# Attention scores of two heads requested together, with the keys' low halves multiplied on 64 partitions each

## The chip, the cores and the metric

One core of one Trainium2 chip runs the whole program as a single launch. The metric is the device time of one execution in microseconds (us). The kernel before was run three times: 1482.33, 1476.66 and 1482.65 us, median 1482.33. One further execution was profiled.

## What is computed

The reference is one step of a two-layer trunk on 128 context tokens and 1024 latent tokens, model width 1024. Each layer normalises, modulates and projects its input, feeds three branches (A attention, B gated mixing, C DeltaNet scan), and projects the joined result back. The change lies in branch A:

```python
def _attend(q, k, v, mask, sink):
    s = jnp.einsum('bqhgd,bkhd->bhgqk', q, k).astype(jnp.float32) * (HEAD_DIM ** -0.5)
    s = jnp.where(mask, s, NEG_INF)
    m = jnp.maximum(jnp.max(s, axis=-1, keepdims=True), sk)   # sk: one logit per head
    p = jnp.exp(s - m)
    p = p / (jnp.sum(p, axis=-1, keepdims=True) + jnp.exp(sk - m))
    return jnp.einsum('bhgqk,bkhd->bqhgd', p.astype(v.dtype), v)
```

There are 8 query heads of 64 dimensions on 2 key heads. A block of 128 latent queries sees its own block of keys, its two neighbours and 128 cached context keys, so up to 512 keys; a context query sees the 128 context keys.

## The kernel before, in words

Tokens are nine tiles of 128 (eight latent, one context, `CTX`). Products that need more than half precision are made from halves: a float32 value is split into a float16 high part and a float16 remainder (the low part).

In `attention`, each key head `kv` and each token tile `t` is a unit. `prep` projects the four query heads of the tile (the helper `proj_tok`, line 170, 24 matmuls for each of queries and gates), rotates them, splits them into halves (ACT copies the high half, line 916, and POOL subtracts for the low half, line 917), and a DMA transposes them (line 919), so that in `qT[:, h, :]` a head's high half stands on partitions 0 to 63 and its low half on 64 to 127. `put_k` has stored the keys the same way but with each half doubled: `Kh` holds the high half on both groups of 64 partitions, `Kl` the low half on both. Hence `qT`·`Kh` over 128 partitions gives (q high + q low)·k high in one matmul, and `qT`·`Kl` gives (q high + q low)·k low.

`heads` takes the four heads in turn. Per head there are one or two blocks of keys (128, or 128 plus 256 or 384), and per block one matmul with `Kh` (line 941) and one with `Kl` (line 942) into the same PSUM bank; head 0 and 2 use bank `b` (`psb`), head 1 and 3 bank `a` (`psa`). Then DVE adds the mask and takes the row maximum (line 946), ACT makes the exponentials (lines 948 and 949), POOL the low half of the probabilities (line 951), and a DMA on SP's queue transposes them (line 953). `weigh` multiplies them with the values five heads later (line 967).

There are two layers, two key heads, nine tiles and four heads: 144 heads, 272 key blocks. The order on each engine is made ahead of time by the tile scheduler, which lists instructions by priority (place in the program) and by when it reckons their inputs ready; each engine then works its list strictly in that order. The program interleaves the attention with the scan of branch C by estimated costs (`merge`). Much of the scan runs on parts of the TensorE array: lines 566 to 597 use 64 by 64 of it, lines 527 and 543 use 32 by 32, and the modulation weights (line 249) use 128 rows by 32 columns. The projections, scores and `weigh` use all 128 by 128.

Of the kernel before, what the change touches and what calls it, by code (L numbers as in the profile page):

```python
# [15 lines left out]
ALU = mybir.AluOpType  # L16
# [30 lines left out]
def hybrid_trunk(  # L47
# [9 lines left out]
    V, S_, G, T = nc.vector, nc.scalar, nc.gpsimd, nc.tensor  # L57
# [8 lines left out]
    def pool(name, bufs=1, side=None):  # L66
        return tc.tile_pool(name=name, bufs=bufs, side=side, reuse_waits="tile")
# [9 lines left out]
    def nm(s):  # L77
        ngen[0] += 1
        return f"{s}_{ngen[0]}"

    def bank(tag, bufs, cols=512, dt=F32):
        return psm.tile([128, cols], dt, tag=tag, name=nm("ps"), bufs=bufs)

    def psp():
        return bank("p", 3)

    def psa(cols=512, dt=F32):
        return bank("a", 1, cols, dt)

    def psb(cols=512, dt=F32):  # L90
        return bank("b", 1, cols, dt)
# [73 lines left out]
    def proj_tok(ps, t, wg, c0=0, n=256):  # L165

        i = 0
        for k in range(8):
            for (a, b) in ((0, 0), (0, 1), (1, 0)):
                T.matmul(ps, X[:, t, k, a, :], wg[:, k, b, c0:c0 + n], start=(i == 0), stop=(i == 23))  # L170
                i += 1
# [691 lines left out]
    def rope_tile(rp, src, nh, rt):  # L863

        n = nh * 64
        a = rp.tile([128, 256], F32, tag="ra", name=nm("ra"), bufs=1)
        u = rp.tile([128, 256], F32, tag="ru", name=nm("ru"), bufs=1)
        s3 = src.rearrange("p (h d) -> p h d", d=64)
        V.tensor_tensor(a[:, 0:n].rearrange("p (h d) -> p h d", d=64), s3, bc(rt[:, 0:64], 1, nh), op=ALU.mult)
        V.tensor_tensor(u[:, 0:n].rearrange("p (h d) -> p h d", d=64), s3, bc(rt[:, 64:128], 1, nh), op=ALU.mult)  # L870
        a4 = a[:, 0:n].rearrange("p (g s f) -> p g s f", s=2, f=16)
        u4 = u[:, 0:n].rearrange("p (g s f) -> p g s f", s=2, f=16)
        V.tensor_tensor(a4[:, :, 0, :], a4[:, :, 0, :], u4[:, :, 1, :], op=ALU.add)
        V.tensor_tensor(a4[:, :, 1, :], a4[:, :, 1, :], u4[:, :, 0, :], op=ALU.add)
        return a

    def attention(l, other=iter(())):
        with pool(f"t3{l}", 1, "right") as p1:
            KT = p1.tile([128, 2, 2, 1280], F16, name="KT")
            Kh, Kl = KT[:, 0], KT[:, 1]  # L880
# [23 lines left out]
            def prep(p2, kv, t, wq, wa):  # L904
                pq = psp()
                proj_tok(pq[:, 0:256], t, wq)
                proj_tok(pq[:, 256:512], t, wa)
                rt = p2.tile([128, 128], F32, tag="rt", name=nm("rt"))
                dma(rt, rope[t])
                qa = rope_tile(p2, pq[:, 0:256], 4, rt)  # L910
                th = p2.tile([128, 256], F32, tag="ga", name=nm("ga"), bufs=5)
                S_.activation(th, pq[:, 256:512], AF.Tanh, scale=IWS * 0.5)
                V.scalar_tensor_tensor(th, th, 1.0, pq[:, 256:512], op0=ALU.add, op1=ALU.mult)
                ql = p2.tile([128, 4, 2, 64], F16, tag="ql", name=nm("ql"))
                q3 = qa.rearrange("p (h d) -> p h d", d=64)
                S_.copy(ql[:, :, 0, :], q3)
                G.tensor_tensor(ql[:, :, 1, :], q3, ql[:, :, 0, :], op=ALU.subtract)
                qT = p2.tile([128, 4, 128], F16, tag="qT", name=nm("qT"), bufs=3)
                turn(qT, ql.rearrange("p h s d -> p (h s d)"))
                return qT, th  # L920

            def heads(p2, prev, kv, t, qT, th):
                if t == CTX:
                    blocks, mk = [(9, 1)], am[:, 0:128]
                else:
                    lo, hi = max(t - 1, 0), min(t + 1, 7)
                    blocks = [(lo, hi - lo + 1), (8, 1)] if t == 0 else [(8, 1), (lo, hi - lo + 1)]
                    mk = am[:, 256:640] if t == 0 else (am[:, 0:384] if t == 7 else am[:, 0:512])
                blist = [b + i for (b, n) in blocks for i in range(n)]
                nk = 128 * len(blist)  # L930
                sm = p2.tile([128, 4], F32, tag="sm", name=nm("sm"), bufs=4)
                nmx = p2.tile([128, 4], F32, tag="nmx", name=nm("nmx"), bufs=4)
                box = []
                for h in range(4):
                    hh = 4 * kv + h
                    ps = psa() if h % 2 else psb()
                    c0 = 0
                    for (b, n) in blocks:
                        cs = slice(c0, c0 + 128 * n)
                        ks = slice(128 * b, 128 * (b + n))  # L940
                        T.matmul(ps[:, cs], qT[:, h, :], Kh[:, kv, ks], start=True, stop=False)  # L941
                        T.matmul(ps[:, cs], qT[:, h, :], Kl[:, kv, ks], start=False, stop=True)  # L942
                        c0 += 128 * n
                    sS = p2.tile([128, 512], F32, tag="sS", name=nm("sS"))
                    P16 = p2.tile([128, 1024], F16, tag="P16", name=nm("P16"), bufs=4)
                    V.tensor_tensor_reduce(sS[:, 0:nk], ps[:, 0:nk], mk, -0.125, nsk[:, hh:hh + 1], ALU.add, ALU.min,  # L946
                                           accum_out=nmx[:, h:h + 1])
                    S_.activation(P16[:, 0:nk], sS[:, 0:nk], AF.Exp, bias=nmx[:, h:h + 1], scale=-1.0)  # L948
                    S_.activation(sS[:, 0:nk], sS[:, 0:nk], AF.Exp, bias=nmx[:, h:h + 1], scale=-1.0,  # L949
                                  accum_out=sm[:, h:h + 1])  # L950
                    G.tensor_tensor(P16[:, nk:2 * nk], sS[:, 0:nk], P16[:, 0:nk], op=ALU.subtract)  # L951
                    PT = p2.tile([128, 8, 128], F16, tag="PT", name=nm("PT"), bufs=AHEAD)
                    turn(PT[:, 0:2 * len(blist), :], P16[:, 0:2 * nk])
                    last = (kv, t, th, sm, nmx) if h == 3 else None
                    pend.append((p2, prev, box, kv, h, blist, PT, last))
                    if len(pend) > AHEAD - 1:
                        weigh(*pend.pop(0))
                    yield 0.95

            def weigh(p2, prev, box, kv, h, blist, PT, last):  # L960

                if not box:
                    box.append(bank("o", 1))
                pops, nb = box[0], len(blist)
                mm = [(0, 0, 128)] + [(j, 1, 64) for j in range(nb)] + [(j, 0, 128) for j in range(1, nb)]
                for i, (j, a, n) in enumerate(mm):
                    T.matmul(pops[:, 128 * h:128 * h + n], PT[:, a * nb + j, :],  # L967
                             Vt[:, blist[j], kv].rearrange("p s d -> p (s d)")[:, 0:n], start=(i == 0), stop=(i == len(mm) - 1))
                if h == 1 and prev:
                    finish(p2, *prev.pop())  # L970
                if last is not None:
                    normal(p2, prev, pops, *last)
# [31 lines left out]
            for kv in range(2):  # L1004
                with pool(f"t3b{l}{kv}", 2, "right") as p2:
                    if kv == 0:
# [7 lines left out]
                        for t in ordert:  # L1014
                            ps = psp()
# [16 lines left out]
                    for i in range(NT + 1):  # L1032
                        if i < NT:
                            ready.append((kv, ordert[i], *prep(p2, kv, ordert[i], wq, wa)))
                            yield 5.2
                        if i > 0:
                            yield from heads(p2, prev, *ready.pop(0))
                            if next(other, None) is not None:
                                yield 3.5
# [104 lines left out]
    for l in range(NL):  # L1144
# [13 lines left out]
        c0 = rs.enter_context(pool(f"c0{l}", 1, "right"))  # L1158
# [116 lines left out]
```

## Time and profile before

| | |
|---|---|
| median of three runs | 1482.33 us (1476.66 to 1482.65) |
| the profiled execution, its own time | 1485.41 us |
| its span, first to last instruction | 1483.6 us |
| mean granted TensorE clock | 0.937 of full speed |
| busy: PE, PEld, DVE, ACT, POOL | 89, 68, 63, 42 and 41% of the span |
| score matmuls, lines 941 and 942 | 272 each, from 243.2 to 1342.1 us |

PE is TensorE's matmul, PEld its weight load. A matmul's shown duration contains its way through the pipeline, so matmuls in a row overlap in the rows; what a matmul costs the engine is the distance from its start to the next one's start. The chain that ended last is followed back from the last instruction; a line's share in it is the time for which that line set the pace.

### The profile page before, as it was taken

The numbers are of one execution on the slowest core, as the hardware profiler recorded it, in microseconds if no ns is written. First come the engines' busy times: TensorE is split into PE (matmuls) and PEld (weight loads), VectorE is DVE, ScalarE is ACT, GpSimd is POOL, SyncE is SP. The second block draws the span as 40 slices with busy tenths as digits, with TensorE's granted clock in tenths as the row PEclk, the third lists the DMA queues.
The fourth block names the chain that finished last, engine by engine and source line by source line (L and its number), as shares of the span: only waits on it lengthen the run. The fifth ranks groups of instructions, "written<-read, shape, count | busy, mean of one in ns | idle before, by whom it ended". The sixth has DMA issues, their size and how long they took to land.

```text
span 1483.6 us, 38268 instructions
## 1 busy us (share of the span) xinstructions
PE 1319.0 (89%) x15479; PEld 1014.8 (68%) x15479; DVE 939.3 (63%) x2230; ACT 618.9 (42%) x1411; POOL 610.7 (41%) x818
## 2 busy tenths in 40 slices
PE   6899989799999699859897999999898769987997
PEld 2765576576768597648786655678787658765786
DVE  3865689885565676554446587687775485666333
ACT  2733444424555226632343444332476313664111
POOL 0751245424655235633232432631667403675200
PEclk8999999997999799969997999999999879998999
DMA  9331045736884218673332122242277212666443
GB/s 362 108 85 47 23 117 112 161 93 151 188 182 93 57 44 150 113 211 78 116 130 78 36 69 60 90 92 51 51 138 132 47 49 69 134 116 169 122 162 107
DMA packets 301564, 162.94 MB, mean 110 GB/s; under 512 B 212622, under 2 KB 277938, under 8 KB 301386
## 3 DMA queue, kind: packets, MB, share of 16 engines
q1 hardware_dynamic: 301261, 160.45, 44.7%
q8 instruction: 122, 2.00, 0.6%
q14 instruction: 56, 0.46, 0.1%
q10 hardware_dynamic: 125, 0.04, 0.0%
HBM read 95.78 MB, written 24.28 MB: 81 GB/s over the span
## 4 chain that ended last, share of the span: by engine, by line
PE 54%; DVE 17%; DMA 13%; issue 7%; POOL 6%; ACT 3%; SPq 1%; DVEq 0%; POOLq 0%; ACTq 0%
PE ps L170 15%; PE ps L1072 12%; PE ps L312 7%; DMA PT<-P 4%; DVE sv L510 2%; DVE sv L512 2%; POOL P L951 2%; PE ps L967 2%; DMA st<-in_w_in_dram 2%; PE ps L249 1%; PE ps L543 1%; DMA st<-in_w_mod_dram 1%; PE ps L527 1%; PE ps L941 1%; DVE y L319 1%
## 5 line engine op out<-in xcount | busy, mean ns | idle before, releaser
L170 PEld LDWEIGHTS <-X 128*128 128x128 f16 x3888 | 349.2, 100 | 106.2 <-issue 43.6
L170 PE MATMUL ps<-wg,X 128*128 128x256 f16 x2592 | 327.3, 279 | 9.1 <-DVE wg L161 3.3
L1072 PEld LDWEIGHTS <-OTm 128*128 128x128 f16 x1728 | 170.0, 100 | 39.9 <-DMA OTm<-mix_d 15.8
L951 POOL TENSOR_TENSOR P<-sS,P 128x512 f16<-128x512 f32 (+2 forms) x144 | 148.9, 1040 | 100.0 <-ACT sS L949 99.4
L1072 PE MATMUL ps<-wo,OTm 128*128 128x256 f16 x1296 | 155.5, 279 | 15.5 <-DMA OTm<-mix_d 14.9
L312 PE MATMUL ps<-X,wg 128*128 128x512 f16 (+1 forms) x864 | 144.8, 326 | 1.8 <-ACT wg L160 1.4
L946 DVE CUSTOM_DVE_ANT_0 sS<-ps,am,nsk 128x512 f32<-128x512 f32 (+2 forms) x144 | 95.0, 670 | 43.7 <-POOL P L951 27.3
L170 PE MATMUL ps<-wb,X 128*128 128x256 f16 x864 | 105.4, 284 | 17.7 <-ACT wb L160 16.8
L312 PEld LDWEIGHTS <-wg 128*128 128x128 f16 x864 | 73.0, 98 | 68.5 <-ACT wg L160 1.8
L948 ACT ACTIVATE P<-sS,nmx 128x512 f16<-128x512 f32 (+2 forms) x144 | 93.4, 659 | 61.5 <-DVE nmx L946 61.0
L949 ACT ACTIVATE sS<-sS,nmx 128x512 f32<-128x512 f32 (+2 forms) x144 | 94.8, 658 | 3.2
L145 POOL TENSOR_TENSOR rs<-ms,mhalf 128x1 f32<-128x1 f32 x36 | 20.6, 574 | 174.8 <-DVE ms L1081 104.3
L967 PE MATMUL ps<-Vt,PT 128*128 128x128 f16 (+1 forms) x992 | 68.2, 212 | 20.7 <-DMA PT<-P 19.6
L319 DVE SCALAR_TENSOR_TENSOR y<-zT,cw,y 128x1156 f32<-128x1156 f32 x48 | 68.9, 1439 | 27.8 <-ACT y L317 27.2
L512 DVE TENSOR_TENSOR sv<-sv 128x31 f32<-128x31 f32 (+15 forms) x186 | 76.2, 410 | 4.2
L967 PEld LDWEIGHTS <-PT 128*128 128x128 f16 x992 | 51.1, 101 | 38.8 <-DMA PT<-P 28.2
L510 DVE TENSOR_TENSOR sv<-sv 128x31 f32<-128x31 f32 (+15 forms) x186 | 74.9, 403 | 4.1
L942 PE MATMUL ps<-KT,qT 128*128 128x128 f16 (+2 forms) x272 | 68.8, 271 | 0.0
L941 PE MATMUL ps<-KT,qT 128*128 128x128 f16 (+2 forms) x272 | 60.6, 273 | 7.1 <-DVE nmx L946 2.9
L1075 ACT ACTIVATE sq<-ps 128x512 f32<-128x512 f32 x36 | 21.4, 595 | 105.8 <-PE ps L1072 64.1
L288 DVE TENSOR_SCALAR hf<-ps,AB 128x128 f32<-128x128 f32 x117 | 39.7, 402 | 39.6 <-PE ps L281 39.5
L161 DVE SCALAR_TENSOR_TENSOR wg<-st,wg 128x1024 f16<-128x1024 f32 x44 | 56.4, 1292 | 12.3 <-ACT wg L160 12.2
(265 smaller groups left out, 2730.0 us busy)
## 6 DMA issues: line engine op xcount, KB each, us to landing
st<-in_w_in_dram SPq DMA_DIRECT2D x40, 512.0 KB
st<-in_w_mod_dram SPq DMA_DIRECT2D x32, 512.0 KB
OTm<-mix_d SPq DMA_DIRECT2D x18, 512.0 KB
wm<-in_w_mod_dram SPq DMA_DIRECT2D x16, 512.0 KB
xt<-in_x_sample_dram SPq DMA_DIRECT2D x16, 512.0 KB
st<-in_w_out_dram SPq DMA_DIRECT2D x16, 512.0 KB
mix_d<-OTA SPq DMA_DIRECT2D x36, 128.0 KB
xs<-xt SPq DMA_DIRECT2D x9, 512.0 KB
```

Of the source, the lines that this page charges most:

```text
L170: T.matmul(ps, X[:, t, k, a, :], wg[:, k, b, c0:c0 + n], start=(i == 0), stop=(i == 23))
L312: T.matmul(ps[:, 0:n], wg[:, k, b, 128 * hg:128 * hg + 128], X[:, t0:t1, k, a, :], start=(i == 0), stop=(i == 23))
L319: V.scalar_tensor_tensor(y, zT[:, tap:tap + 1156], cw[:, tap * 6 + ct:tap * 6 + ct + 1], y, op0=ALU.mult, op1=ALU.add)
L510: V.tensor_tensor(t3, m3[:, 0:m, m:m + 1].to_broadcast([128, m, w]), y3[:, m:m + 1, m:32].to_broadcast([128, m, w]), op=ALU.mult)
L512: V.tensor_tensor(y3[:, 0:m, m:32], y3[:, 0:m, m:32], t3, op=ALU.subtract)
L941: T.matmul(ps[:, cs], qT[:, h, :], Kh[:, kv, ks], start=True, stop=False)
L946: V.tensor_tensor_reduce(sS[:, 0:nk], ps[:, 0:nk], mk, -0.125, nsk[:, hh:hh + 1], ALU.add, ALU.min, accum_out=nmx[:, h:h + 1])
L948: S_.activation(P16[:, 0:nk], sS[:, 0:nk], AF.Exp, bias=nmx[:, h:h + 1], scale=-1.0)
L949: S_.activation(sS[:, 0:nk], sS[:, 0:nk], AF.Exp, bias=nmx[:, h:h + 1], scale=-1.0, accum_out=sm[:, h:h + 1])
L951: G.tensor_tensor(P16[:, nk:2 * nk], sS[:, 0:nk], P16[:, 0:nk], op=ALU.subtract)
L967: T.matmul(pops[:, 128 * h:128 * h + n], PT[:, a * nb + j, :], Vt[:, blist[j], kv].rearrange("p s d -> p (s d)")[:, 0:n], start=(i == 0), ...
L1072: T.matmul(ps[:, 256 * i:256 * i + 256], OTm[:, k, a, :], w[:, k, b, :], start=(n == 0), stop=(n == 23))
```

## The change

The scores of heads `h` and `h + 1` are now written together for `h` = 0 and 2, both PSUM banks taken at once. The products with the keys' high halves stay as they are, over 128 partitions. The product with the low halves now takes q high alone: head `h` uses partitions 0 to 63, head `h + 1` partitions 64 to 127, so that each occupies half the rows of the array and all of its columns (64 by 128). For that the odd heads' halves are stored the other way round in `ql`, so line 916's one copy and line 917's one subtraction become two each, half as wide. The product of q low with k low is left out.

```diff
-                S_.copy(ql[:, :, 0, :], q3)
-                G.tensor_tensor(ql[:, :, 1, :], q3, ql[:, :, 0, :], op=ALU.subtract)
+                for i in range(2):
+                    S_.copy(ql[:, i::2, i, :], q3[:, i::2])
+                    G.tensor_tensor(ql[:, i::2, 1 - i, :], q3[:, i::2], ql[:, i::2, i, :], op=ALU.subtract)
...
-                    ps = psa() if h % 2 else psb()
-                    c0 = 0
-                    for (b, n) in blocks:
-                        cs = slice(c0, c0 + 128 * n)
-                        ks = slice(128 * b, 128 * (b + n))
-                        T.matmul(ps[:, cs], qT[:, h, :], Kh[:, kv, ks], start=True, stop=False)
-                        T.matmul(ps[:, cs], qT[:, h, :], Kl[:, kv, ks], start=False, stop=True)
-                        c0 += 128 * n
+                    if h % 2 == 0:
+                        pss = [psb(), psa()]
+                        c0 = 0
+                        for (b, n) in blocks:
+                            cs = slice(c0, c0 + 128 * n)
+                            ks = slice(128 * b, 128 * (b + n))
+                            for i in range(2):
+                                T.matmul(pss[i][:, cs], qT[:, h + i, :], Kh[:, kv, ks], start=True, stop=False)
+                            for i in range(2):
+                                hf = slice(64 * i, 64 * i + 64)
+                                T.matmul(pss[i][:, cs], qT[hf, h + i, :], Kl[hf, kv, ks], start=False, stop=True)
+                            c0 += 128 * n
+                    ps = pss[h % 2]
```

The scheduler places these matmuls one by one, and what it makes of a pair is seen in TensorE's order. First place: layer 0, a latent tile with key blocks of 128 and 384. Before, one head's scores stand so (line 941 is the high product, 942 the low one, `ps` the PSUM bank of the head):

```order
L941 LDWEIGHTS qT_4855
L941 MATMUL ps_5373<-KT,qT_4855 128x128
L942 LDWEIGHTS qT_4855
L942 MATMUL ps_5373<-KT,qT_4855 128x128
L941 LDWEIGHTS qT_4855
L941 MATMUL ps_5373<-KT,qT_4855 128x384
L942 LDWEIGHTS qT_4855
L942 MATMUL ps_5373<-KT,qT_4855 128x384
```

The same tile in the changed kernel (line 944 is the high product, 947 the low one on 64 rows, 973 is `weigh`): the end of the pair's first head, and the start of its second.

```order
L944 MATMUL ps_5389<-KT,qT_4869 128x384
L947 LDWEIGHTS qT_4869
L947 MATMUL ps_5389<-KT,qT_4869 128x384
L973 LDWEIGHTS PT_5035
L973 MATMUL ps_5354<-Vt,PT_5035 128x128
L973 LDWEIGHTS PT_5062
L973 MATMUL ps_5354<-Vt,PT_5062 128x128
L973 LDWEIGHTS PT_5062
L973 MATMUL ps_5354<-Vt,PT_5062 128x64
L944 LDWEIGHTS qT_4869
L944 MATMUL ps_5390<-KT,qT_4869 128x128
L947 LDWEIGHTS qT_4869
```

The two heads of the pair (`ps_5389`, `ps_5390`) stand apart, and inside each the high and low products alternate as before; only the low one's shape in the array is new.

Second place: layer 0, a latent tile with key blocks of 256 and 128. Before, two heads followed each other directly; the first of them:

```order
L941 LDWEIGHTS qT_6413
L941 MATMUL ps_6660<-KT,qT_6413 128x256
L942 LDWEIGHTS qT_6413
L942 MATMUL ps_6660<-KT,qT_6413 128x256
L941 LDWEIGHTS qT_6413
L941 MATMUL ps_6660<-KT,qT_6413 128x128
L942 LDWEIGHTS qT_6413
L942 MATMUL ps_6660<-KT,qT_6413 128x128
```

In the changed kernel the pair is kept together here:

```order
L944 LDWEIGHTS qT_6435
L944 MATMUL ps_6684<-KT,qT_6435 128x256
L944 LDWEIGHTS qT_6435
L944 MATMUL ps_6685<-KT,qT_6435 128x256
L947 LDWEIGHTS qT_6435
L947 MATMUL ps_6684<-KT,qT_6435 128x256
L947 LDWEIGHTS qT_6435
L947 MATMUL ps_6685<-KT,qT_6435 128x256
```

Here the low products of both heads stand side by side, as the source writes them.

Over TensorE's whole order, the 272 low products form 246 runs: 26 of two (15 with 128 keys, 3 with 256, 8 with 384) and 220 of one. The number of places where a matmul uses another part of the array than the matmul ahead of it (128 by 128, 64 by 128, 64 by 64, 128 by 32, 32 by 32) goes from 519 to 958. Matmul counts are equal; ACT and POOL have 36 more instructions each. The order of other work around the scores is shifted too, on every engine, from the first attention tile on.

## Rows read from the trace of the kernel before

**Rows 1.** The page, part 1: busy time and share of the span.
```profile
PE 1319.0 (89%) x15479; PEld 1014.8 (68%) x15479; DVE 939.3 (63%) x2230; ACT 618.9 (42%) x1411; POOL 610.7 (41%) x818
```

**Rows 2.** The page, part 4: the chain that ended last, by engine.
```profile
PE 54%; DVE 17%; DMA 13%; issue 7%; POOL 6%; ACT 3%; SPq 1%; DVEq 0%; POOLq 0%; ACTq 0%
```

**Rows 3.** Busy time over four stretches (243-500, 540-640, 1020-1160, 1240-1345 us): their sum.
```profile
sum 602.00, PE 547.16 PEld 428.37 DVE 403.47 ACT 317.30 POOL 334.69; mean PE 136.79 PEld 107.09 DVE 100.87 ACT 79.33 POOL 83.67
```

**Rows 4.** The chain by line in each of the four stretches, in their order.
```profile
by line: PE ps L170 18.6%; PE ps L249 7.9%; DMA st<-in_w_mod_dram 7.7%; issue 5.2%; DVE sv L510 4.4%; DMA PT<-P 4.2%; PE ps L967 4.0%; DVE sv L512 3.7%; DMA qT<-ql 3.2%; PE ps L941 3.1%; PE ps L543 2.8%; PE ps L942 2.7%; PE ps L449 2.2%; PE
by line: PE ps L170 17.4%; DMA PT<-P 14.4%; issue 10.0%; DMA st<-in_w_out_dram 8.7%; POOL P L951 8.3%; PE ps L543 4.0%; PE ps L527 3.9%; PE ps L967 2.6%; PE ps L566 2.3%; PE ps L941 2.2%; POOL qk L556 2.0%; SPq L953 1.9%; PE ps L942 1.7%; A
by line: DMA PT<-P 12.2%; issue 9.9%; PE ps L170 9.3%; DVE sv L512 9.0%; POOL P L951 6.3%; DVE sv L510 5.6%; PE ps L967 4.4%; PE ps L527 3.7%; PE ps L941 2.8%; PE ps L543 2.8%; DVE sS L946 2.5%; PE ps L942 2.4%; POOL gt L433 2.2%; PE ps L44
by line: PE ps L170 18.6%; DMA PT<-P 14.6%; issue 8.6%; POOL P L951 6.3%; PE ps L967 4.9%; PE ps L543 3.8%; PE ps L527 3.8%; PE ps L941 3.7%; DVE sS L946 2.9%; PE ps L942 2.9%; ACT P L948 2.6%; PE ps L566 2.2%; ACT sS L949 1.7%; PE ps L582 
```

**Rows 5.** Groups by shape, line 942's (line 941's counts are the same).
```profile
L942 PE MATMUL ps<-KT,qT 128*128 128x384 f16 x96 | 32.6, 341 | 0.0
L942 PE MATMUL ps<-KT,qT 128*128 128x128 f16 x144 | 32.1, 224 | 0.0
L942 PE MATMUL ps<-KT,qT 128*128 128x256 f16 x32 | 8.7, 272 | 0.0
```

**Rows 6.** Timeline of PE from 398.9 us: start, us, instruction; array part rows*columns.
```profile
398.91 0.22 PE L941 MATMUL ps<-KT,qT 128*128 128x128 f16 x1
398.96 0.22 PE L942 MATMUL ps<-KT,qT 128*128 128x128 f16 x1
399.02 0.33 PE L941 MATMUL ps<-KT,qT 128*128 128x384 f16 x1
399.18 0.33 PE L942 MATMUL ps<-KT,qT 128*128 128x384 f16 x1
399.34 1.04 PE L170 MATMUL ps<-wg,X 128*128 128x256 f16 x8
400.22 0.27 PE L437 MATMUL ps<-gt,triL 128*128 128x128 f16 x2
```

**Rows 7.** Timeline of PE and PEld from 1272.9 us.
```profile
1272.95 0.33 PE L942 MATMUL ps<-KT,qT 128*128 128x384 f16 x1
1273.21 0.27 PE L566 MATMUL ps<-ident,qk 64*64 64x64 f32 x1
1273.22 0.27 PE L593 MATMUL ps<-vn,kd 64*64 64x64 f32 x1
...
1273.20 0.13 PEld L566 LDWEIGHTS ps<-ident,qk 64*64 64x64 f32 x1 [0.32 <-issue]
```

**Rows 8.** Timeline of PE from 393.9 us, and from 475.8 us.
```profile
393.90 0.33 PE L942 MATMUL ps<-KT,qT 128*128 128x384 f16 x1
394.16 1.04 PE L249 MATMUL ps<-st,csp 128*32 128x512 f32 x2
...
475.94 0.33 PE L583 MATMUL ps<-S,qw 64*64 64x64 f32 x4
...
476.05 0.22 PE L583 MATMUL ps<-S,qw 64*64 64x64 f32 x1
476.20 0.34 PE L942 MATMUL ps<-KT,qT 128*128 128x384 f16 x1
```

**Rows 9.** Groups by shape: line 917's and 916's, and half-width instructions on POOL and ACT.
```profile
L917 POOL TENSOR_TENSOR ql<-ra,ql 128x256 f16<-128x256 f32 x36 | 26.1, 726 | 43.2 <-ACT ql L916 38.8 <-issue 4.4
L558 POOL TENSOR_TENSOR kd<-cqk,kdf 128x128 f32<-128x128 f32 x72 | 32.0, 445 | 55.9 <-PE ps L593 55.4
L916 ACT CAST ql<-ra 128x256 f16<-128x256 f32 x36 | 14.4, 401 | 7.5 <-DVE ra L874 6.4 <-issue 0.3
L604 ACT COPY oacc<-ps 128x128 f32<-128x128 f32 x36 | 9.4, 260 | 4.8 <-DVE S L601 4.3
```

**Rows 10.** Who waited for lines 941 and 942.
```profile
DVE sS L946: 14.1, 12
```

## The prediction, made before the changed kernel ran

> **What bounds the kernel now.** I read the page's busy times first. TensorE's matmuls are busy for 89% of the span, no other engine for more than 63% [rows 1]. Busy matmuls overlap in the pipeline, so that share alone doesn't say that TensorE sets the pace; the chain does: 54% of it is PE, the rest is spread over DVE, DMA, POOL and waits of the issue kind [rows 2]. Then I asked where the scores stand. Nearly all score matmuls lie in four stretches of 257, 100, 140 and 105 us, 602 us together, in which PE is busy 547 us [rows 3]. So 55 us without any matmul is the most that these stretches offer to swallow more matmul time.
>
> In the same stretches I read the chain by line [rows 4]. The low products (line 942) have 2.7, 1.7, 2.4 and 2.9% of it: 6.9 + 1.7 + 3.4 + 3.0 = 15.0 us. The high ones (line 941) have 3.1, 2.2, 2.8 and 3.7%: 8.0 + 2.2 + 3.9 + 3.9 = 18.0 us. To see which part of their work that is I need what a score matmul costs TensorE, and that is the step from one start to the next. For 128 keys it is 398.91 to 399.02 us over two, 0.055; for 384 keys 399.18 to 399.34, 0.16; for 256 columns eight take 0.88, 0.11 each [rows 6]. With the counts of the low products, 96 x 0.16 + 32 x 0.11 + 144 x 0.055 = 15.4 + 3.5 + 7.9 = 26.8 us [rows 5], and the high ones as much. Of these 53.6 us the chain holds 33.0: **62% of score time on TensorE is on the path.** The rest is hidden behind the softmax (POOL's line 951, the transposing DMA of `P`) and the scan's DVE work, which hold large shares of their own [rows 4]. I use this 62% for whatever the change adds to or takes from the scores' time on TensorE.
>
> **The change part by part.**
>
> *Products side by side.* Two low products on different halves of the array's rows can run together. The trace has nothing in 64 by 128, but it has 64 by 64: the matmuls of lines 566 and 593 start at 1273.21 and 1273.22 us, 0.01 apart [rows 7]. I take it that two row halves with all columns can do it too. If all 136 pairs of blocks did, half of 26.8 us would go, 13.4 us on TensorE. But the scheduler leaves only 26 pairs together (both places of the order above show the two cases). These save 15 x 0.055 + 3 x 0.11 + 8 x 0.16 = 2.4 us. A low product that stands alone saves nothing: it streams the same number of keys, now through half of the rows.
>
> *Changing the part of the array.* This is the term that decides. When the next matmul uses the same part as the last, the step is that of the columns: 0.16 us after 384 keys [rows 6]. When it uses another, the step is longer. From 1272.95 (384 keys on 128*128) the next start, on 64*64, is 1273.21: 0.26 us [rows 7]. From 393.90 (again 384) to a matmul on 128*32 at 394.16: 0.26 us [rows 8]. Both are 0.10 us more than 0.16. The way back costs about the same: four matmuls on 64*64 start between 475.94 and 476.05, so a step of a pair there is at most 0.055, but the 128*128 matmul behind them starts 0.15 later, at 476.20 [rows 8]: 0.095 more. I use 0.095 for all. In the first case the weights of the next part begin to load at 1273.20 [rows 7], that is only when the streaming has ended and that extra time is over, while in an unchanged sequence they are loaded early and cost nothing. So the price doesn't hang on how large the weights are or on their type, and three kinds of change have it alike. For a change into or out of 64 by 128, which no row shows, the bounds are 0 (a change of rows alone is free) and 0.10; I take the 0.095 of its three neighbours.
>
> The Trainium skill, page TensorEngine Tiling (Array Packing), section Key Properties, says that to change the tiling mode, as against the tile alone, drains TensorE. It speaks against this change. The trace agrees, with 0.095 us for each of its three kinds. The same page's Theoretical Speedup gives up to 2x where the contraction is 64 or less. By that alone the low products would halve and the time would fall by the 8.3 us of the second rival below, since it counts neither the split pairs nor the drains.
>
> The order has 958 such places where it had 519. The 439 new ones are nearly all at the scores: 246 runs of low products, each entered and left, 492, less those where another change stood there anyway. 439 x 0.095 = 41.7 us more on TensorE. A head with two key blocks has four more changes, and three of them come before its last product, so its maximum on DVE starts 0.285 us later.
>
> *Two copies and two subtractions for one.* ACT: 2 x 0.260 for 0.401 us, 36 times, +4.3 us; POOL: 2 x 0.445 for 0.726, +5.9 us [rows 9]. The second copy runs beside the first subtraction. From the first copy to the end of the second subtraction is then 0.260 + 2 x 0.445 = 1.15 us against 0.401 + 0.726 = 1.13, so the transposing DMA behind them starts 0.02 us later, 0.8 us over 36. ACT and POOL have room here, busy 317 and 335 of 602 us [rows 3]. I take 0; if none of it were hidden it would be 10.
>
> *Banks taken in pairs.* The first head's scores no longer wait for their own bank alone in the program's text, but the scheduler's split order lets each head start when its own bank is free, so I take 0. Where a pair is kept together its second high product waits for the earlier head's line 946 and holds up the rest of TensorE's list behind it; that happens in 26 of 136 places, and DVE's pass over 512 keys is short beside the ACT and POOL work per head that sets the pace there. DVE's own wait for the scores is 14.1 us over 12 waits [rows 10]; that is all that an earlier start could give back.
>
> **Sum.** +41.7 - 2.4 = 39.3 us on TensorE; 62% of it on the path: +24.4 us. Against the profiled execution's own 1485.4 us (its span is 1483.6) that is 1510; that execution is 3.1 us above the median of the three runs, so for the median I say **1507 us**. If all 39.3 reach the path, 1522, and if the preparation's 10 do too, 1532. If the 55 us without a matmul swallow nearly all, 1483.
>
> **The rivals.**
>
> *The slack takes it.* The same drains, but most fall where the softmax or a DMA sets the pace: the chain's shares of `DMA PT<-P` are 12 to 15% in three of four stretches. With 0 to 15% reaching the path the time is 1482 to 1488. Against it: the low products themselves are on the path for 15.0 of 26.8 us, 56%, and the drains sit right beside them.
>
> *No drain for a change of rows alone.* Then the saving is what is left: with the pairs as they are split, 2.4 x 0.62 = 1.5 us, 1481. If the pairs had also stayed whole, 13.4 x 0.62 = 8.3 us, 1474, but the order shows that they don't: **the change for the most part doesn't do what it says.** For it: no 64 by 128 row exists. Against it: the three kinds of change that do exist cost alike, 128*32 with all its rows in use among them.
>
> *Faster, on the other side.* The whole order has shifted, and scores of a second head are asked for earlier. If this took away all of DVE's 14.1 us of waiting for the scores [rows 10] and the drains put no more than 15% of their 41.7, 6 us, on the path, the time would be 8 us less, 1474. It decides only there: with more than 6.7 us of drains on the path, 14.1 us don't make up for them by 0.5%, and I expect 26. For it: a pair's scores are requested ahead of the first head's softmax in the program. Against it: in the split order the second head isn't.
>
> *More than the sum.* The scores' delay of 0.285 us per two-block head comes back in each round of the softmax and TensorE's list stalls for late DVE and POOL results besides: 1522 to 1532.
>
> **How the numbers follow.** 0.5% is 7.4 us, about what a measurement of this kernel can tell from no change, so "same" is 1475 to 1490. Forecast (1490 to 1522): 0.68. More than the sum (over 1522): 0.11, half of it over 1526. Slack takes it: 0.09, nearly all in "same". No drain: 0.07, two parts in "same" to one below it by the shifted order. Faster by the order: 0.05. That makes slower 0.79, same 0.14, faster 0.07. From 1484 to 1526 lie the forecast, half of what is above it and half of the slack case: 0.68 + 0.055 + 0.05, about 0.8.
>
> **What would show it.** In the changed profile's timeline: 0.26 us from a high product with 384 keys to a low one and back where it was 0.16, with the weights of the low one loading late; where the low products of a pair stand together, their starts within 0.01 us. In the chain: scores with some 20 us more than 33. The four stretches should be longer, and the output projections between and after them unchanged. I am wrong if the steps stay 0.16 (no drain), if they are 0.26 but the stretches don't grow (slack), or if the time grows where no scores are (the shifted order).

## The result, and the profile after

The changed kernel took 1504.12 us in the median (1492.74 to 1507.97, 4 runs) against 1482.49 before: ratio 1.0135, interval 1.0103 to 1.0166, slower by 21.6 us. Timed again beside the last experiments it gave 1498.81 against 1483.92, 14.9 us more, ratio 1.0116 (1.0075 to 1.0157). Losses in us are differences of medians all through; a ratio and its interval are worked out from all runs and need not be the quotient of the medians (here 1.0100). The forecast was 1507, with 1484 to 1526 around it.

The page of the changed kernel, part 1 and the first line of part 4:

```profile
PE 1368.8 (91%) x15479; PEld 1025.0 (68%) x15479; DVE 937.2 (62%) x2230; ACT 618.5 (41%) x1447; POOL 620.6 (41%) x854
PE 56%; DVE 14%; DMA 13%; issue 6%; POOL 5%; ACT 4%; SPq 2%; DVEq 0%; POOLq 0%; ACTq 0%
```

TensorE has as many matmuls as before [rows 1], but 50 us more of busy time. DVE and ACT are unchanged, POOL has 10 us more, and PE's share of the chain went from 54 to 56% [rows 2].

What a head costs on TensorE now, in the changed kernel's timeline of PE, and PEld behind it:

```profile
1292.25 0.22 PE L944 MATMUL ps<-KT,qT 128*128 128x128 f16 x1
1292.41 0.23 PE L947 MATMUL ps<-KT,qT 64*128 64x128 f16 x1
1292.57 0.34 PE L944 MATMUL ps<-KT,qT 128*128 128x384 f16 x1
1292.83 0.33 PE L947 MATMUL ps<-KT,qT 64*128 64x384 f16 x1
1293.10 0.37 PE L973 MATMUL ps<-Vt,PT 128*128 128x128 f16 x5
...
1292.40 0.09 PEld L947 LDWEIGHTS <-qT 64*128 64x128 f16 x1 [0.16 <-issue]
```

Read the starts. 0.16 us after 128 keys where it was 0.055, and 0.26 to 0.27 after 384 where it was 0.16 [rows 6]; the head takes 0.85 us of TensorE, from 1292.25 to 1293.10, where it took 0.43, from 398.91 to 399.34. The low product's weights begin to load 0.01 us before it starts, and not while the product ahead of it streams. Each of the four changes of the array's part costs 0.10 to 0.11 us, into 64 by 128 and out of it.

Where the scheduler left a pair together, the same view shows:

```profile
609.10 0.50 PE L944 MATMUL ps<-KT,qT 128*128 128x384 f16 x2
609.53 0.34 PE L947 MATMUL ps<-KT,qT 64*128 64x384 f16 x2
609.79 0.40 PE L973 MATMUL ps<-Vt,PT 128*128 128x128 f16 x6
```

Two low products with 384 keys take 0.26 us together to the next start, as long as one alone above, and both lie in 0.34 us, where one alone takes 0.33. They do run side by side.

Where the time went was first read in the two stretches from a layer's first score to the first matmul of its output projection: start:end and length, then busy time of PE, PEld, DVE, ACT and POOL, granted clock, DMA share, GB/s. Before:

```profile
243.20:664.70 421.50, 365.29 (x4953) 279.82 (x4952) 282.69 (x738) 188.97 (x462) 195.44 (x271) 0.91 0.61 131
1027.90:1361.40 333.50, 289.46 (x4344) 240.92 (x4341) 226.89 (x611) 167.57 (x419) 184.61 (x257) 0.93 0.47 93
```

The changed kernel:

```profile
242.50:670.00 427.50, 389.29 (x4978) 283.47 (x4977) 281.00 (x735) 187.01 (x477) 201.37 (x289) 0.92 0.55 122
1031.70:1390.10 358.40, 324.80 (x4403) 254.00 (x4401) 229.87 (x620) 170.51 (x439) 189.44 (x276) 0.88 0.48 95
```

The changed kernel, profiled a second time:

```profile
242.90:669.20 426.30, 383.76 (x4978) 280.29 (x4976) 282.66 (x740) 187.52 (x478) 202.54 (x290) 0.93 0.56 123
1031.20:1380.10 348.90, 313.98 (x4403) 246.00 (x4400) 229.69 (x618) 170.19 (x439) 189.26 (x276) 0.91 0.48 96
```

Of the 439 new changes of the array's part 220 stand in layer 0 and 219 in layer 1, some 22 us of TensorE in each. Against the kernel before, layer 0's stretch grew by 6.0 and 4.8 us and layer 1's by 24.9 and 15.4, which looks as if nearly all of the loss were in layer 1. But the stretches don't hold the same work: 59 more matmuls stand in layer 1's and 25 more in layer 0's, because the paired order moved them there. A better base is the first experiment below, which has the pairs with every low product on all rows. TensorE's order in its trace, of 15479 matmuls, differs from that of the change's two profiles in 22 and 6 places, and these two differ from each other in 16: it is the same order. Its two stretches hold as many matmuls but for one in each:

```profile
243.60:661.80 418.20, 365.81 (x4977) 277.46 (x4974) 283.95 (x737) 186.66 (x477) 200.51 (x288) 0.93 0.57 125
1022.10:1367.40 345.30, 294.71 (x4402) 245.28 (x4400) 227.52 (x620) 169.76 (x439) 191.09 (x276) 0.92 0.49 98
```

Against this, layer 0 grew by 9.3 and 8.1 us and layer 1 by 13.1 and 3.6. Both layers let a part of their 22 us through, and these single executions don't show that one lets through more than the other. In layer 1 the granted clock is 0.88 and 0.91 where it is 0.92 without the 64 rows. The granted clock has two levels here, 1.2 and 2.4 GHz, so over 358.4 and 348.9 us these means are some 86 and 63 us at the lower one. Work at half the speed loses half of that time, so the 23 us between the two executions of the one program are worth up to 11 us, as an estimate; they differ by 9.5.

### The profile page after: what moved, and what is told of

Its sections match the earlier page's. It is cut to its first block, busy times and chain, and to the rows that moved or that the text cites. A ratio compares the mean times of both kernels' runs of the same rounds, so it can differ in the third digit from the quotient of the medians.

```text
span 1505.8 us, 38337 instructions
## 1 busy us (share of the span) xinstructions
PE 1368.8 (91%) x15479; PEld 1025.0 (68%) x15479; DVE 937.2 (62%) x2230; ACT 618.5 (41%) x1447; POOL 620.6 (41%) x854
## 4 chain that ended last, share of the span: by engine, by line
PE 56%; DVE 14%; DMA 13%; issue 6%; POOL 5%; ACT 4%; SPq 2%; DVEq 0%; POOLq 0%; ACTq 0%
PE ps L170 16%; PE ps L1078 12%; PE ps L312 6%; DMA PT<-P 4%; DMA st<-in_w_in_dram 2%; PE ps L973 2%; PE ps L947 2%; PE ps L944 2%; DMA st<-in_w_mod_dram 2%; POOL P L957 2%; PE ps L543 1%; DVE y L319 1%; PE ps L249 1%; DVE sv L510 1%; PE ps L527 1%
## 5 line engine op out<-in xcount | busy, mean ns | idle before, releaser
L170 PE MATMUL ps<-wg,X 128*128 128x256 f16 x2592 | 333.9, 282 | 12.9 <-DVE wg L161 3.7
L319 DVE SCALAR_TENSOR_TENSOR y<-zT,cw,y 128x1156 f32<-128x1156 f32 x48 | 68.9, 1439 | 27.4 <-ACT y L317 26.8
L944 PE MATMUL ps<-KT,qT 128*128 128x128 f16 (+2 forms) x272 | 72.6, 283 | 3.6 <-DVE nmx L952 1.9
L947 PE MATMUL ps<-KT,qT 64*128 64x128 f16 (+2 forms) x272 | 69.4, 282 | 0.0
```

The source lines that it names most:

```text
L319: V.scalar_tensor_tensor(y, zT[:, tap:tap + 1156], cw[:, tap * 6 + ct:tap * 6 + ct + 1], y, op0=ALU.mult, op1=ALU.add)
L944: T.matmul(pss[i][:, cs], qT[:, h + i, :], Kh[:, kv, ks], start=True, stop=False)
L947: T.matmul(pss[i][:, cs], qT[hf, h + i, :], Kl[hf, kv, ks], start=False, stop=True)
```

## The experiments

The main theory: each change of the part of the array in use costs TensorE 0.10 us, and the changed kernel has 439 more of them. Its rivals: taking two heads and two banks together costs; the preparation in two halves costs; the shifted order of all other work costs; or the pairs lose only because the scheduler splits them. A last question was which part of time added at the scores reaches the end. Each kernel below was timed beside the kernel before, on the same chip as it.

**Pairs, with the low products on all rows** (`e1_pair_full`). The change, but:

```diff
-    T.matmul(pss[i][:, cs], qT[hf, h + i, :], Kl[hf, kv, ks], start=False, stop=True)
+    T.matmul(pss[i][:, cs], qT[:, h + i, :], Kl[:, kv, ks], start=False, stop=True)
```

> The changed kernel, pairs and banks and the two copies as in it, but the low products again over all 128 rows of the array. Changes of the array's part in TensorE's order: 510, where before has 519 and the change 958. If the drains make the loss (main theory, about 0.10 us for each change, 62% on the path): 1482 us, ratio to before 1.000 within 0.005. If taking two heads and both banks together, the copies, or the shifted order make it: 1504 us as with the change, ratio about 1.0135.

1480.22 us, ratio 0.9978 (0.9952 to 1.0005). With everything of the change in place but the 64 rows, and in the same order on TensorE, the loss is gone. Pairing, banks, copies and the shifted order don't make it.

**Single heads, with the low products on 64 rows** (`e2_half_solo`). The kernel before, but:

```diff
-    T.matmul(ps[:, cs], qT[:, h, :], Kl[:, kv, ks], start=False, stop=True)
+    T.matmul(ps[:, cs], qT[0:64, h, :], Kl[0:64, kv, ks], start=False, stop=True)
```

> The kernel before, heads one by one as in it, with only the low product taken on 64 partitions (partitions 0 to 63 for every head; q low times k low left out). 1006 changes of the array's part, 487 more than before, and no two low products side by side. Drains: 487 x 0.10 x 0.62 = +30 us, 1512, ratio 1.020. If pairing, banks, copies or order made the loss: 1482, ratio 1.000.

1519.82 us, ratio 1.024 (1.0207 to 1.0272): 36.8 us slower, more than the change itself and more than the 30 expected. The 64 rows do it with no pair in the program. 36.8 of 48.7 us is 76%.

**The same for every second head** (`e10_half_even`).

```diff
+    lo = slice(0, 128) if h % 2 else slice(0, 64)
-    T.matmul(ps[:, cs], qT[:, h, :], Kl[:, kv, ks], start=False, stop=True)
+    T.matmul(ps[:, cs], qT[lo, h, :], Kl[lo, kv, ks], start=False, stop=True)
```

> The kernel before, heads one by one, with the low product on 64 rows for the even heads alone (q low times k low left out there). 750 changes of the array's part: 231 more than before, 47% of the 487 of the run in which all heads had it. Drains: 47% of that run's +36.5 us: +17, 1500, ratio 1.0115, and the mean granted clock between the two (0.939 and 0.931). If the loss were in the order of other work or came at once with the first such product: not in proportion.

1500.91 us, ratio 1.0127 (1.0087 to 1.0166): 17.0 us for 231 changes, where 487 gave 36.8. That is 0.074 and 0.076 us for each: in proportion to their number, within wide intervals. The mean granted clock was 0.9335, between the two as expected.

**No low products** (`e4_no_low`). The kernel before without line 942.

> The kernel before without the low products (q times k low is left out): 26.8 us less on TensorE at the same places, 498 changes of the array's part. It measures which part of score time on TensorE is on the path. Main theory, 62%: -17 us, 1465, ratio 0.988. If the softmax's chain hides it (slack): 1478 to 1482, ratio 0.997 to 1.0. If all of it counts: 1455, ratio 0.982.

1474.49 us, ratio 0.9957 (0.993 to 0.9983): 8.5 us less for 26.8 us of matmuls, 32%; the interval is 2.5 to 10.4 us, 9 to 39%. The chain's 62% is out. The full slack, 0.997 to 1.0, isn't: the interval reaches into it.

**Low products made twice** (`e7_low_twice`).

```diff
-    T.matmul(ps[:, cs], qT[:, h, :], Kl[:, kv, ks], start=False, stop=True)
+    T.matmul(ps[:, cs], qT[:, h, :], Kl[:, kv, ks], start=False, stop=False)
+    T.matmul(ps[:, cs], qT[:, h, :], Kl[:, kv, ks], start=False, stop=True)
```

> The kernel before with every low product made twice over 128 rows, added twice (so the scores count q times k low twice): +26.8 us on TensorE at the same places, with no new change of the array's part. If time added at the scores reaches the path as the drains of the change did, 52%: +14, 1496, ratio 1.0094. If as the removal of the low products showed, 32%: +8.5, 1491, ratio 1.0057. If 62%, as worked out from the chain: +16.6, 1499, ratio 1.011. If drains cost more than their steps show, this one stays well below the change's loss per us.

1478.46 us, ratio 0.9971 (0.9941 to 1.0001). All three shares fail: 26.8 us more of streaming on TensorE at the scores cost nothing. Its profile's two stretches, from the first score to the output projection:

```profile
243.40:669.10 425.70, 372.89 (x5114) 285.63 (x5112) 283.31 (x740) 189.59 (x463) 195.97 (x273) 0.94 0.58 129
1024.00:1358.70 334.70, 298.24 (x4522) 250.64 (x4520) 227.80 (x619) 166.87 (x420) 187.18 (x260) 0.94 0.51 95
```

They are 4.2 and 1.2 us longer than before's, with the clock at 0.94 in both where it was 0.91 and 0.93. Besides the 136 added products each holds other matmuls more than before, 25 and 42, and the rest of the profiled execution is 14.2 us shorter, so the stretches alone don't tell what the added work cost. Over its 12 runs the mean granted clock was 0.9485, in the 35 runs of before beside it 0.9391. Within this kernel's runs, 0.01 more clock went with some 12 us less, so 0.0094 would be 11 us, an estimate. This kernel, with more streaming, was granted more clock, and that may have paid for a part of its extra work; it is read from a correlation and wasn't tried by itself.

**The preparation alone** (`e5_prep_split`). The kernel before with the change's two copies and two subtractions.

> The kernel before with only the preparation of the change: two copies and two subtractions of half the width, the odd heads' halves the other way round; heads one by one, low products over all 128 rows. Main theory: hidden, at most 0.8 us, 1482, ratio 1.000. If the preparation were a part of the loss: up to 10 us, 1492, ratio 1.007.

1483.49 us, ratio 0.9999 (0.9976 to 1.0023). It is hidden, as reckoned.

**Pairs held by a critical section** (`e3_pair_kept`).

```diff
+    with tc.tile_critical():
         for i in range(2):
             T.matmul(pss[i][:, cs], qT[:, h + i, :], Kh[:, kv, ks], start=True, stop=False)
         for i in range(2):
             hf = slice(64 * i, 64 * i + 64)
             T.matmul(pss[i][:, cs], qT[hf, h + i, :], Kl[hf, kv, ks], start=False, stop=True)
```

> The changed kernel with the two high and two low products of each key block held together in TensorE's order, so that all 136 pairs of low products stand side by side, as the source reads. 745 changes of the array's part, 226 more than before. Drains with the whole saving: (226 x 0.10 - 13.4) x 0.62 = +5.7 us, 1488, ratio 1.004. If pairs and banks taken together cost, more than the change itself: 1504 or above, ratio 1.0135 or more. If the drains cost nothing: 1474, ratio 0.994.

1762.84 us, ratio 1.1889 (1.1847 to 1.1931). This says nothing on the change, since the sections cost so much more than it. From the waits (who waited for what, us in total, times, longest; line 945 is here the high product, 953 the mask and row maximum):

```profile
DVE sS L953 <- PEq L943: 221.1, 64, 10.1
PEld ps L945 <- issue: 200.9, 137, 6.5
```

TensorE's weight loads stand still for 1.5 us ahead of each of some 136 sections. The pairs had to be held another way.

**Pairs held by edges, block by block** (`e3_pair_edges`, `e9_pairs_whole`). An edge in the scheduler alone, which orders two instructions of one engine and waits for nothing. In the first kernel the low products follow the second head's high one, in the other both heads' high ones. This is the second; the first has the one edge alone:

```diff
...
-    T.matmul(pss[i][:, cs], qT[:, h + i, :], Kh[:, kv, ks], start=True, stop=False)
+    his[i] = T.matmul(pss[i][:, cs], qT[:, h + i, :], Kh[:, kv, ks], start=True, stop=False)
...
+    with tc.issue_after(his[0].ins), tc.issue_after(his[1].ins):
         for i in range(2):
             hf = slice(64 * i, 64 * i + 64)
             T.matmul(pss[i][:, cs], qT[hf, h + i, :], Kl[hf, kv, ks], start=False, stop=True)
```

> The changed kernel in which the low products of a key block may not stand ahead of the second head's high one: 90 of 136 pairs of low products side by side instead of 26, 827 changes of the array's part. Drains: 308 x 0.10 - 8.7 = +22 us on TensorE, 52% of it +11.5, 1494, ratio 1.008: between the grouped order and the change. If it is the order of other work: no relation with the count of changes.

1489.26 us, ratio 1.0046 (1.0023 to 1.007).

> The changed kernel with every pair of low products side by side, block by block, as its source reads: no low product of a block may stand ahead of either head's high one. 766 changes of the array's part, 13.4 us saved. Drains: 247 x 0.10 - 13.4 = +11 us on TensorE, about half of it on the path: 1489, ratio 1.004. If the change lost only because its pairs were split: at or below before, ratio 0.996 or less. If waiting for both banks costs by itself: 1495 or more, ratio 1.008 or more.

1483.65 us, ratio 1.0009 (0.9985 to 1.0034). With 135 of 136 pairs side by side, as the source reads, the loss is gone, but nothing is won: the 247 more changes cost TensorE 24.7 us and the pairs save some 13. The 11 us that are left don't show in the time; the interval reaches to 5. With one edge 90 pairs stay together. It leaves a pair free to part where the second head's scores come first, since that head's low product then needn't wait for the other head; how often that is the reason isn't shown.

**Grouped by pair** (`e6_pair_grouped`, `e8_grouped_whole`). All high products of both heads first, then all low ones; held by one edge, and by both, which is shown.

```diff
...
-                            for i in range(2):
-                                T.matmul(pss[i][:, cs], qT[:, h + i, :], Kh[:, kv, ks], start=True, stop=False)
+                            for i in range(2):
+                                his[i] = T.matmul(pss[i][:, cs], qT[:, h + i, :], Kh[:, kv, ks], start=(c0 == 0), stop=False)
+                            c0 += 128 * n
+                        c0 = 0
+                        with tc.issue_after(his[0].ins), tc.issue_after(his[1].ins):
+                            for (b, n) in blocks:
...
                                 for i in range(2):
                                     hf = slice(64 * i, 64 * i + 64)
-                                    T.matmul(pss[i][:, cs], qT[hf, h + i, :], Kl[hf, kv, ks], start=False, stop=True)
+                                    T.matmul(pss[i][:, cs], qT[hf, h + i, :], Kl[hf, kv, ks], start=False, stop=(c0 + 128 * n == nk))
```

> The changed kernel with a pair's products in another order: the high ones of both heads and all blocks first, then the low ones of both heads and all blocks, which may not stand ahead of the last high one. 689 changes of the array's part (958 with the change, 519 before); low products stand side by side more often, which saves some 8 us on TensorE. Drains: 170 x 0.10 - 8 = +9 us on TensorE; with the share that the change itself showed (21.6 of 41.5 us, 52%) +5, 1487, ratio 1.003. If asking for two heads together costs by itself: 1500 or more. If the loss comes from the order of other work: no relation with the count of changes.

1477.05 us, ratio 0.9954 (0.9929 to 0.9979): the fastest with the 64 rows, ahead of both kernels. Its mean granted clock was 0.9467, against 0.9391 for before beside it; within its runs and before's 0.01 went with 10 and 6 us, so its whole lead of 6.3 us may be clock.

> The grouped order with the pairs held whole: no low product of a pair may stand ahead of either head's last high one. 624 changes of the array's part, nearly all low products side by side (13.3 us saved on TensorE). Drains against saving: 105 x 0.10 - 13.3 = -3 us on TensorE, about half of it on the path: 1482, ratio 0.999; the looser grouped order (689 changes) gave 0.9954. If a head's scores suffer when they must wait for the other head's bank: 1490 or more, ratio 1.005 or more.

1480.15 us, ratio 0.9983 (0.9955 to 1.001). Fewer changes than the looser order and no better; the intervals overlap, and the two aren't told apart.

**The change once more** (`after_again`).

> The changed kernel once more, beside the others on one chip, for a narrower interval: 1504 us, ratio 1.0135 (1.010 to 1.017), mean granted clock below that of before.

1498.81 us, ratio 1.0116 (1.0075 to 1.0157): inside the first interval. But its mean granted clock, 0.9427, was not below that of before, 0.9393: I expected that wrongly. Here the drains cost their time without a lower clock over the whole program.

All together, by changes of the array's part, with TensorE's net cost (0.10 us for each change over 519, less what stands side by side) and the ratio:

| kernel | changes | net us on TensorE | ratio |
|---|---|---|---|
| pairs, all rows | 510 | -1 | 0.9978 |
| grouped, held whole | 624 | -3 | 0.9983 |
| grouped | 689 | +9 | 0.9954 |
| pairs held whole | 766 | +11 | 1.0009 |
| pairs, one edge | 827 | +22 | 1.0046 |
| every second single head | 750 | +23 | 1.0127 |
| the change | 958 | +42 | 1.0135 and 1.0116 |
| all single heads | 1006 | +49 | 1.024 |

Within the paired kernels the time rises with the net cost but for the grouped one, and within the single heads too. At the same net cost, 22 and 23 us, the paired kernel loses 6 us and the single one 17. Their mean granted clocks differ in the same direction, 0.9402 and 0.9335, and within each kernel's runs 0.01 went with 8 and 6 us, so some 4 to 6 of the 11 us may be clock. What gives the rest isn't shown.

## Why the prediction was right

**The price of a change of the array's part.** I took 0.095 us for 64 by 128 from three neighbours, none of which cut the rows alone; it is 0.10 both ways, at the size that I took. The rival in which rows alone are free is out: the steps show it, and the single heads lose 76% of the sum with nothing else changed in the source. The Trainium skill, page TensorEngine Tiling (Array Packing), section Key Properties, says that changing the tiling mode drains TensorE; the trace agrees, now for a row half as well, with 0.10 us.

**The split pairs.** The order as built decided. With 26 of 136 pairs side by side the kernel loses 1.35%; with 135 of them it is level, and grouped a little ahead. So "the change for the most part doesn't do what it says" was right of the pairs. But there it stood under the rival without drains, and that was too narrow: with drains the split is most of the loss, since the held pairs cost 1.0009.

**Preparation and banks.** Taken as 0, measured as ratios of 0.9999 and 0.9978. POOL's time grew by 9.9 us and not by 5.9, and was hidden all the same.

**The share that reaches the end: 62%.** This is the term that was mis-sized. I read from the chain what part of score time is on the path and used it for all that is added or removed. The runs gave 32% for removing 26.8 us and less than nothing for adding as much of streaming. For the drains, against 41.5 us, the change gave 21.6 and in the repeat 14.9, 52 and 36%; single heads 74 and 76%. The cleanest pair of kernels is the change and the pairs with all rows, alike but for the rows and in one order on TensorE: ratios of 1.0135 and 1.0116 against 0.9978, 20 to 23 us, about half of the 42 us between them. So +24.4 came out near +21.6 in part by luck: one share was used for whatever is added or removed, and for work at the same places it lay anywhere between nothing and three quarters. No step of the prediction told drains from streaming, or pairs from single heads. The chain shows what ended last, not what would have ended last in its place. In layer 0 of the kernel before, the chain by line over 625 to 665 us, the end of the stretch, reads:

```profile
by line: DMA st<-in_w_out_dram 13.5%; DMA mix_d<-oc 13.0%; issue 12.4%; DMA OTm<-mix_d 8.9%; DMA PT<-P 7.1%; DVE wg L161 5.5%; DMA Sx<-S 3.4%; DVE wo L161 3.1%; ACT wg L160 2.7%; SPq L743 2.5%; POOL P L951 2.3%; DVE oa L991 2.3%; DVE of L75
```

There transfers of the output weights and of the scan's results hold the largest shares, and no line of TensorE is among those shown. Such an end may have swallowed drains that stand ahead of it, of which 8 to 9 of 22 us came through in this layer; that the transfers are the reason wasn't tried.

**What the profile should show.** The steps of 0.26 and the late weights came, and the side-by-side pairs too. The part behind layer 1's stretch was to be unchanged, but took 115.7 and 114.4 us where it had taken 122.2. With the low products on all rows it takes 115.9, so that is the paired order, in which 58 matmuls fewer stand there, and not the drains. The scores' part of the chain I put at some 20 us over 33; the chain by line of the changed kernel begins

```profile
by line: PE ps L170 16.5%; PE ps L1078 11.7%; issue 6.0%; PE ps L312 5.8%; DMA PT<-P 3.6%; DMA st<-in_w_in_dram 2.5%; PE ps L973 2.3%; PE ps L947 2.2%; PE ps L944 2.1%; DMA st<-in_w_mod_dram 1.9%; POOL P L957 1.5%; PE ps L543 1.5%; DVE y L3
```

so lines 947 and 944 have 4.3% of 1505.8 us, 65 us, 32 more; the time grew by less, since other lines left the chain in turn.

**Left open.** Why 41.5 us of drains cost 15 to 22 while 26.8 us of streaming cost nothing. One reason may be the scheduler, which can set other work around matmuls that it reckons with, and the drains may not be in its reckoning; another is the clock, 0.9485 with more streaming. Neither was tried by itself. The kernels without low products and with twice as many also have another order of the rest of the work on TensorE than the kernel before.

## What to carry to other kernels

Before a matmul is cut to half of the array's rows, count in the built order how often TensorE changes the part of the array that it uses, and price each change from a step in the trace (0.10 us here): two halves side by side save one streaming, 0.055 to 0.16 us, and a visit costs two changes, so by these prices only several such products in one visit pay; the grouped kernels, with up to four, came out from level to 0.5% ahead. Source lines that stand together are not instructions that stand together; when a gain needs neighbours, look at the order and hold them with scheduler edges, not with a critical section. Compare stretches between kernels that hold the same work in the same order: here that was the paired kernel with all rows, and against the kernel before the loss seemed to lie in another place. And a line's share of the chain bounds neither what its removal gives nor what an addition costs: time a kernel with the work removed and one with it doubled.

## What the runs showed of the hardware that I had not expected

A row half with all 128 columns pays the same 0.10 us as a part with fewer columns. At the lower clock level, 1.2 GHz, the price is about the same. Two places where the granted clock is 0.50, in the kernel before and in the changed one:

```profile
365.08 0.53 PE L941 MATMUL ps<-KT,qT 128*128 128x384 f16 x1
365.40 0.53 PE L942 MATMUL ps<-KT,qT 128*128 128x384 f16 x1
365.72 0.85 PE L967 MATMUL ps<-Vt,PT 128*128 128x128 f16 x8
...
1350.93 0.50 PE L944 MATMUL ps<-KT,qT 128*128 128x384 f16 x1
1351.37 0.50 PE L947 MATMUL ps<-KT,qT 64*128 64x384 f16 x1
1351.80 0.40 PE L973 MATMUL ps<-Vt,PT 128*128 128x128 f16 x3
```

A step after 384 keys is 0.32 us without a change, twice the 0.16 of the full clock, and 0.43 to 0.44 with one, so a change adds 0.11 to 0.12.

Two such halves start as one: the 26 pairs that stand together start 3 to 4 ns apart, and two low products of 384 keys lie in 0.34 us. The Trainium skill, page TensorE: Matmul & The Clock Gate, Part 3, says that tiles in different row groups start about 4 ns apart; the trace agrees.

The mean granted clock was 0.9485 with the low products twice, 0.9391 before, 0.937 without them, and 0.9308 with 49 us of drains in single heads. But the pairs on all rows had 0.9443 with no more streaming, and the change in its second series 0.9427 with 42 us of drains, so neither streaming nor drains alone set it.
